# Fewer mixing steps in the second MLP's first chunk, a second load of the output blocks from SP, and a norm and two subtractions rewritten

## The chip, the cores and the metric

The kernel runs as one program on one core of a Trainium2 chip. The metric is the device time of one execution in microseconds (us); smaller is better. The engines are TensorE (PE for matmuls, PEld for its weight loads), VectorE (DVE), ScalarE (ACT), GpSimd (POOL) and SyncE (SP). DMAs are issued from SP, ACT and POOL.

## The reference

One inference step of a two-layer encoder on 512 prompt tokens and 64 sample tokens, which the kernel treats as 576 columns of one matrix with 1024 features:

```python
for i in range(2):
    h = rmsnorm(x, norm_mix[i])
    y = pool_mixer(h) if i == 0 else sparse_attention(h) @ w_o   # layer 0 pools, layer 1 attends
    x = x + y
    h = rmsnorm(x, norm_mlp[i])
    u = relu(h @ w_up[i])                # 1024 -> 4096
    x = x + (u * u) @ w_down[i]          # 4096 -> 1024
y = rmsnorm(x, norm_final)
```

Everything is float32. The two MLPs hold most of the arithmetic; the attention picks 128 or 144 keys of each query by an indexer score.

## The kernel before, in words

**Data.** `x` stays in SBUF as 8 tiles of 128 features by 576 tokens. Each float32 operand of a matmul is split into an upper part (a cast to fp32r) and a lower part (value minus upper part), and each product is three matmuls: upper by upper, upper by lower, lower by upper. A matmul takes 288 tokens (half of 576) as its moving side.

**Weights.** A weight block is a 128 by 1024 tile. `load` (L145) brings it into a staging tile `raw` of 512 KB, `split_block` casts it on ACT (L204) and subtracts on DVE or, in parts of the attention, on POOL (L205), into one of three weight tiles `w`. A `raw` tile comes free when that subtraction is done. There are two `raw` tiles, and two more in the MLPs. The list `jobs` sets the order of the loads. Loads of MLP weights are issued by SP; loads of the attention's input blocks (`in_w_in`) and output blocks (`in_w_o`) by ACT, in the order of ACT's other work.

**The MLPs.** The 4096 hidden features are handled in 4 chunks of 1024. For a chunk `c`, four `up(c, q)` calls each make two tiles of hidden features; `up(c + 1, 0)` is done ahead; then four `DownPair` calls each add two output tiles to `x`. Both the down products of most chunks and the up products of the second MLP from chunk 1 on use a seven-product scheme (Strassen-like) in place of eight. It needs sums of weight quarters. `factors` (L594 on) makes the sums of the activations. The weight sums of the first MLP are made by POOL (L278 to L283) when the block arrives; those of the second MLP are made ahead of time in DRAM, by `mixing()`.

**Mixing.** `mixing()` (L215 on) is a generator. It fills the DRAM tile `mixed` with the weight sums in 12 groups that start three steps apart; each group needs four plain copies from SP (L240: two from the weights, then two from `mixed`) and four accumulating DMAs from POOL (L234), each of 512 KB. The whole takes 3 x 12 + 9 = 45 steps. A step is taken wherever the code says `next(mixes, None)`: in the first MLP twice in each `up` with q = 1 and q = 2 and once in each DownPair with q = 1 to 3, which is 4 x (4 + 3) = 28 steps; in the second MLP six times in chunk 0's `up` calls (twice for each of q = 1, 2, 3), then once in each later `up` and in every second DownPair. The copies of a step are ordered behind the last SP load that was recorded ahead of them.

**The norms.** `Norm.stats` sums the squares over features by small matmuls (L369), and takes a square root (ACT, L388) and a reciprocal with a correction (DVE, L390 to L395) to get one factor per token; `Norm.spread` spreads the factors over the partitions: a diagonal on DVE (L359, L362), two matmuls (L349), two copies on ACT (L350) into `rbm`. The first hidden tiles wait in PSUM until `rbm` is there, and are then taken out by L713. In the first MLP `stats` stands behind the second up tile and `spread` behind the third; in the second MLP `stats` stands between the two tiles and `spread` behind the second. Matmuls at L688 then zero the two `seed` banks.

**Output blocks.** `w_o` is passed over twice: in the first pass a quarter of the tokens' products is made while the attention is still running, in the second pass (L319 on tile `wo`) the other 320 columns. Each pass loads all 8 blocks.

**Order of the work.** The program is handed to a scheduler that lays the instructions of each engine out in a fixed order before launch, by a model of its own; each engine then runs its list in that order and waits where an operand is not there.

Of the kernel before, what the change touches and what calls it, by code (L numbers as in the profile page):

```python
# [12 lines left out]
ALU = mybir.AluOpType  # L13
# [28 lines left out]
FACTORS = ("b11", "b22", "b21", "t3", "t1", "t2", "t4")  # L42
PLAIN = ((4, 4, 4, 4), (4, 0, 0, 0))
AHEAD = 2
BLOCKS = 3
VS = 2

# [2 lines left out]
def pool_dsa_kernel(ctx: ExitStack, tc: tile.TileContext, a, o):  # L50
# [114 lines left out]
    def mlp_jobs(layer, strassen, plain):  # L165
        down = a["w_down"][layer]

        def ups(c, ps):
            for q in ps:
                if q < plain[c]:  # L170
                    jobs.extend(("mlp", f) for f in rows("up", layer, c, q))
                else:
                    jobs.append(("made", "up", c, q))

        for c in range(4):
            ups(c, range(c > 0, 4))
            if c < 3:
                ups(c + 1, range(1))
            if c >= strassen:
                jobs.extend(("mlp", down[c, m]) for m in range(KT))  # L180
            elif layer:
                jobs.extend(("made", "down", c, q) for q in range(KT // 2))
            else:
                jobs.extend(("pair", *rows("down", layer, c, q)) for q in range(KT // 2))

    mlp_jobs(0, 4, PLAIN[0])
    jobs.extend(("w_in", a["w_in"][j]) for j in range(2))
    jobs.extend(("w_v", a["w_v"][j]) for j in range(2))
    jobs.extend(("w_in", a["w_in"][j]) for j in range(2, 15))
    for _ in range(2):  # L190
        jobs.extend(("w_o", a["w_o"][m]) for m in range(KT))
    mlp_jobs(1, 3, PLAIN[1])
    ready = []
    how = {"sub": dve}
# [50 lines left out]
    def loaded():  # L245

        waiting, held = [], 0
        while jobs or waiting:
            while jobs and held < LOADS_AHEAD["more" in phase] and ("last" in phase or jobs[0][0] not in ("pair", "made")):
                kind, *srcs = jobs.pop(0)  # L250
                if kind == "made":
                    r1, r2 = rows(srcs[0], 1, *srcs[1:])
                    m = mixed[:, pairs[tuple(srcs)]].rearrange("p a b -> p (a b)")
                    srcs = [r1, m[:, 1024:], m[:, :1024], r2[:, 512:]]
                mlp = kind in ("mlp", "pair", "made")
                waiting.append((kind, [load(src, src.shape[1], nc.sync if mlp else act, mlp)[:, :src.shape[1]] for src in srcs]))
                held += len(srcs)
            kind, tiles = waiting.pop(0)
            held -= len(tiles)
            yield kind, tiles  # L260
# [243 lines left out]
    def mlp(layer, gi, strassen, order=range(KT), end=None):  # L504
# [63 lines left out]
                dve.tensor_tensor(bx[j][:, 5:7, 1], t[:, 2:4], f32(bx[j][:, 5:7, 0]), ALU.subtract)  # L568
                yield

        def up_plain(order):
            w = next_block()
            pt = [psum1("up", "pd" if "pd" in phase and not ups else "po") for _ in range(2)]
            ups.append(pt)
            for n, k in enumerate(order):
                for i, (part, wt) in enumerate(((0, 0), (1, 0), (0, 1))):
                    for h in range(2):
                        pe.matmul(pt[h][:, :HT], w[:, wt, k * P:(k + 1) * P], moving(k, part, h),  # L578
                                  start=n == 0 and i == 0, stop=n == KT - 1 and i == 2)
            return pt  # L580
# [12 lines left out]
        def factors(v, u):  # L593
# [12 lines left out]
                return  # L606
            act.copy(u[:, 0:3, 0], v[:, 1:4])
            dve.tensor_tensor(u[:, 0:3, 1], v[:, 1:4], f32(u[:, 0:3, 0]), ALU.subtract)
            dve.tensor_tensor(b11, b11, b12, ALU.subtract)
            dve.tensor_tensor(b12, b12, b22, ALU.subtract)  # L610
            dve.tensor_tensor(b22, b22, b11, ALU.add)
            dve.tensor_tensor(b21, b21, b22, ALU.subtract)
            act.copy(u[:, 3:7, 0], v)
# [79 lines left out]
        def up(c, q):  # L693
# [30 lines left out]
            v = None  # L724
            if first:
                pts = []
                for i in range(2):
                    pts.append(up_plain(order))
                    if i == 1 - layer:
                        norm.stats(banks[0])  # L730
                late.append(pts)
                if layer:
                    spread()
                return
            for i in range(2):
                pt = up_plain(range(KT))
                if late:
                    spread()
                if not i:
                    v = new_v()  # L740
                evacuated(i, pt)
                if layer or q in (1, 2):
                    next(mixes, None)
                if layer:
                    with tc.issue_after(last_of["diag"].ins), tc.issue_after(last_of["rt"].ins):
                        next(mixed, None)
                if not layer and (c, q) == (3, 3):
                    us[c][q] = us[c][q] or u_tile()
                    factors_by_tile(i, v, us[c][q])
# [7 lines left out]
        for c in range(4):  # L757
            for q in range(c > 0, 4):
                up(c, q)
            if c < 3:  # L760
                up(c + 1, 0)
            if c < strassen:
                for q in range(KT // 2):
                    if q % 2 if layer else q:
                        next(mixes, None)
                    pair = DownPair(q, us[c], seeded(), layer > 0)
                    pair.opening(c == 3 and q == 0)
                    pair.closing((c, q) != (3, 3))
                continue
# [793 lines left out]
```

## Time and profile before

| | us |
|---|---|
| median of 3 runs | 1120.58 |
| lowest, highest of them | 1118.39, 1123.9 |
| the profiled execution | 1127.65 |
| its span, first to last instruction | 1125.9 |
| PE busy in the span | 1091.3 (97%) |
| DVE, ACT, POOL busy | 790.7, 557.7, 293.6 |

In the span of the profiled execution the up matmuls of the first MLP run from 36 to 387 us, the attention's input projections from about 440 on, the second pass of the output blocks from 694 to 726 us, and the second MLP from 726 us to the end; the up matmuls of its first chunk end at 779 us. A view of stretches gives the busy time of each engine in each stretch, and then the clock that was granted to TensorE as a share of full speed, the busy share of the 16 DMA engines, and what they moved in GB/s.

### The profile page before, as it was taken

The page shows a single profiled execution, that of the slowest core. Times are in us where ns is not written, and L with a number is a line of the kernel's source. Part 1 is how long each engine was busy: PE and PEld are TensorE (multiplying, and loading weights), DVE is VectorE, ACT ScalarE, POOL GpSimd, SP SyncE. Part 2 cuts the span into 40 slices and gives each one's busy share as a digit, 9 for nine tenths or more (in the row PEclk, how much of TensorE's full clock was granted, in tenths as well). Part 3 has the DMA queues.
Part 4 walks back from the last instruction along what each step waited for, and adds up shares of the span by engine and source line. Part 5 has one row for each costly group of instructions (what it writes and reads, how often), then busy time and mean ns, then how long its engine had stood idle before and what let it go on. Part 6 is the DMA issues. An engine that isn't in the chain of part 4 may idle for free. (4 is left out here: it accounts for less than half of the span.)

```text
span 1125.9 us, 20515 instructions
## 1 busy us (share of the span) xinstructions
PE 1091.3 (97%) x8118; PEld 1073.9 (95%) x8118; DVE 790.7 (70%) x1448; ACT 557.7 (50%) x937; POOL 293.6 (26%) x227
## 2 busy tenths in 40 slices
PE   9999999999999999999899999999899999999995
PEld 8999999999999999999789998999799999999995
DVE  7767656766755886659999942887567867865644
ACT  8534334334434454435387654655436636644542
POOL 3004414431351560147973440002000000000002
PEclk9999999999999999999999997999999999999997
DMA  6264488389469867457642341458977565555402
GB/s 218 61 177 105 129 225 237 90 225 256 117 158 263 215 184 235 119 144 194 196 118 67 118 128 37 146 154 241 274 208 213 167 199 161 167 154 174 141 20 84
DMA packets 80208, 183.52 MB, mean 163 GB/s; under 512 B 10753, under 2 KB 22320, under 8 KB 80112
## 3 DMA queue, kind: packets, MB, share of 16 engines
q1 hardware_dynamic: 62304, 139.71, 38.6%
q0 software_dynamic: 13056, 25.17, 13.7%
q10 hardware_dynamic: 4752, 17.34, 5.0%
q8 instruction: 64, 1.05, 0.4%
q14 instruction: 32, 0.26, 0.1%
HBM read 167.10 MB, written 61.22 MB: 203 GB/s over the span
## 5 line engine op out<-in xcount | busy, mean ns | idle before, releaser
L204 ACT CAST w<-raw 128x1024 fp32r<-128x1024 f32 (+2 forms) x242 | 211.2, 890 | 234.4 <-PE seed L422 73.8
L205 DVE TENSOR_TENSOR w<-raw,w 128x1024 fp32r<-128x1024 f32 (+2 forms) x224 | 244.6, 1099 | 68.9 <-ACT w L204 68.6
L578 PE MATMUL up<-xs,w 128*128 128x288 f32 x1536 | 205.8, 295 | 0.5 <-DVE v L713 0.5
L578 PEld LDWEIGHTS up<-xs,w 128*128 128x128 f32 x1536 | 203.8, 188 | 0.9 <-DVE v L713 0.9
L422 PE MATMUL seed<-u,w 128*128 128x288 f32 x1008 | 146.7, 296 | 2.1 <-ACT seed L447 1.2
L422 PEld LDWEIGHTS seed<-u,w 128*128 128x128 f32 x1008 | 138.2, 188 | 3.5 <-ACT seed L447 1.9
L422 PE MATMUL a<-u,w 128*128 128x288 f32 x672 | 101.5, 298 | 6.2 <-ACT w L204 4.5
L422 PE MATMUL c<-u,w 128*128 128x288 f32 x672 | 100.7, 297 | 2.0 <-DVE w L205 1.2
L422 PEld LDWEIGHTS a<-u,w 128*128 128x128 f32 x672 | 93.8, 189 | 8.0 <-ACT w L204 5.4
L422 PEld LDWEIGHTS c<-u,w 128*128 128x128 f32 x672 | 93.1, 188 | 3.2 <-DVE w L205 1.7
L319 PE MATMUL pj<-xs,w 128*128 128x288 f32 x672 | 92.8, 294 | 0.0
L319 PEld LDWEIGHTS pj<-xs,w 128*128 128x128 f32 x672 | 90.4, 188 | 0.7
L234 POOL DMA_DIRECT2D mixed<-in_w_down x24 | 27.6, 1196 | 173.2 <-DMA mixed<-mixed 128.7
L234 POOL DMA_DIRECT2D mixed<-in_w_up x24 | 27.5, 1207 | 140.6 <-DMA mixed<-mixed 121.3
L422 PE MATMUL seed<-bx,w 128*128 128x288 f32 x432 | 63.0, 298 | 0.0
L807 POOL TENSOR_TENSOR x<-x,spare 128x320 f32<-128x320 f32 (+1 forms) x9 | 8.2, 945 | 208.8 <-ACT spare L803 208.8
L422 PEld LDWEIGHTS seed<-bx,w 128*128 128x128 f32 x432 | 59.9, 190 | 0.1
L205 DVE TENSOR_TENSOR w<-sum,w 128x1024 fp32r<-128x1024 f32 (+1 forms) x32 | 33.4, 1044 | 33.1 <-ACT w L204 33.1
L278 POOL TENSOR_TENSOR sum<-raw 128x512 f32<-128x512 f32 x16 | 23.5, 1470 | 123.4 <-DMA raw<-in_w_down 123.4
L319 PE MATMUL dn<-u,w 128*128 128x288 f32 (+2 forms) x384 | 51.7, 295 | 0.0
L713 DVE SCALAR_TENSOR_TENSOR v<-up,rbm 128x288 f32<-128x288 f32 x80 | 32.5, 450 | 27.2 <-PE up L578 27.1
L319 PEld LDWEIGHTS dn<-u,w 128*128 128x128 f32 x384 | 51.0, 188 | 0.2
(292 smaller groups left out, 1974.6 us busy)
## 6 DMA issues: line engine op xcount, KB each, us to landing
raw<-in_w_up SPq DMA_DIRECT2D x52, 512.0 KB, 4.6
raw<-in_w_down SPq DMA_DIRECT2D x52, 512.0 KB, 4.5
raw<-mixed SPq DMA_DIRECT2D x48, 512.0 KB, 4.1
mixed<-in_w_down POOLq DMA_DIRECT2D x24, 512.0 KB, 7.6
mixed<-mixed SPq DMA_DIRECT2D x24, 512.0 KB, 7.9
mixed<-in_w_up POOLq DMA_DIRECT2D x24, 512.0 KB, 10.0
raw<-in_w_o ACTq DMA_DIRECT2D x16, 512.0 KB, 3.6
raw<-in_w_in ACTq DMA_DIRECT2D x15, 512.0 KB, 4.3
```

Of the source, the lines that this page charges most:

```text
L204: act.copy(w[:, 0, at], src[:, at])
L205: how["sub"].tensor_tensor(w[:, 1, at], src[:, at], f32(w[:, 0, at]), ALU.subtract)
L234: pool.dma_start(to, add, accum_op=ALU.add)
L278: pool.tensor_tensor(s[:, :512], r2[:, :512], r2[:, 512:], ALU.add)
L319: pe.matmul(pt[h][:, :m] if isinstance(pt, tuple) else pt[:, h, :m], wt, xs[k][:, part, c:c + m], start=(k == ks[0] and i == 0), stop=(k = ...
L422: pe.matmul(bank[:, :HT], wt[:, at], ut, start=first and j == 0 and i == 0, stop=j == 3 and i == 2, skip_group_check=True)
L578: pe.matmul(pt[h][:, :HT], w[:, wt, k * P:(k + 1) * P], moving(k, part, h), start=n == 0 and i == 0, stop=n == KT - 1 and i == 2)
L713: dve.scalar_tensor_tensor(v[:, 2 * i + h], pt[h][:, :HT], 0.0, halves(norm.rb)[:, h], ALU.max, ALU.mult)
L807: pool.tensor_tensor(x[k][:, t], x[k][:, t], rb, ALU.mult)
```

## The change

It has five parts.

- In `up`, a step of mixing is taken once in every plain `up` with q = 1, 2 or 3, and once more with q = 1 and 2 in the first MLP only. The first MLP has 4 x (5 + 3) = 32 steps in place of 28, the second MLP's first chunk three in place of six in its `up` calls. The 45 steps in all stay.
- The second pass of the output blocks has a kind of its own, `w_o2`, whose loads are issued by SP.
- `stats` now stands in the second up tile of both MLPs (ahead of its fourth of 8 parts in the first MLP, ahead of its first in the second MLP), and `spread` behind that tile in both.
- In `factors` of the second MLP, `b11 -= b12` and `b12 -= b22` are one instruction on a view of two tiles.
- The place of `up(c + 1, 0)` comes from a table, `UP_BEFORE`, whose entries name the place at which it stood.

```diff
+UP_BEFORE = ((0, 0, 0, None), (0, 0, 0))
+STATS = (3, 0)
...
-    for _ in range(2):
-        jobs.extend(("w_o", a["w_o"][m]) for m in range(KT))
+    for kind in ("w_o", "w_o2"):
+        jobs.extend((kind, a["w_o"][m]) for m in range(KT))
...
-                mlp = kind in ("mlp", "pair", "made")
+                mlp = kind in ("mlp", "pair", "made", "w_o2")
...
+                if between and n == between[0]:
+                    between[1]()
...
-            dve.tensor_tensor(b11, b11, b12, ALU.subtract)
-            dve.tensor_tensor(b12, b12, b22, ALU.subtract)
+            back, ahead = (bass.AP(t.tensor, t.offset, [t.ap[0], (step * HT, 2), t.ap[1]]) for t, step in ((b11, -1), (b12, 2)))
+            dve.tensor_tensor(back, back, ahead, ALU.subtract)
...
+                stats = lambda: norm.stats(banks[0])
                 for i in range(2):
-                    pts.append(up_plain(order))
-                    if i == 1 - layer:
-                        norm.stats(banks[0])
+                    pts.append(up_plain(order, (STATS[layer], stats) if i else None))
                 late.append(pts)
-                if layer:
-                    spread()
+                spread()
...
-                if late:
-                    spread()
...
-                if layer or q in (1, 2):
+                if (i == 0 and q) or (not layer and q in (1, 2)):
                     next(mixes, None)
```

Three places show what the scheduler made of it. Rows give the line, the operation, and output and inputs; the changed kernel's line numbers are one to three off.

**SP and POOL, the second MLP's first chunk.** SP before, from the last load for `up(1, 0)` to the first down pair's loads (`raw` is a staging tile, `mixed` the DRAM tile):

```order
L145 DMA raw_8560<-in_w_up 128x512
L240 DMA mixed<-mixed 128x2x512
L240 DMA mixed<-in_w_up 128x2x512 x2
L240 DMA mixed<-mixed 128x2x512 x2
L240 DMA mixed<-in_w_up 128x2x512 x2
L145 DMA raw_8989<-mixed 128x1024
L145 DMA raw_8985<-in_w_down 128x1024
L145 DMA raw_8987<-mixed 128x1024
L240 DMA mixed<-mixed 128x2x512
```

The same stretch of SP with the change:

```order
L147 DMA raw_8569<-in_w_up 128x512
L241 DMA mixed<-in_w_up 128x2x512 x2
L241 DMA mixed<-mixed 128x2x512 x2
L147 DMA raw_8987<-mixed 128x1024
L147 DMA raw_8983<-in_w_down 128x1024
L147 DMA raw_8985<-mixed 128x1024
L147 DMA raw_8989<-in_w_down 128x512
```

Four copies stand ahead of the first down pair's loads in place of seven, and none between its loads. POOL before, from the end of the attention to the last norm:

```order
L1447 TENSOR_TENSOR x_7967<-x_7967,wo_7323 128x256 x2
L234 DMA mixed<-in_w_down 128x2x512 x2
L234 DMA mixed<-in_w_up 128x2x512 x3
L234 DMA mixed<-in_w_down 128x2x512
L234 DMA mixed<-in_w_up 128x2x512 x7
L807 TENSOR_TENSOR x_7964<-x_7964,spare_11802 128x320 x2
```

With the change:

```order
L308 TENSOR_TENSOR ck_7799<-raw_7801,ck_7799 128x512
L1446 TENSOR_TENSOR x_7978<-x_7978,wo_7334 128x256 x2
L235 DMA mixed<-in_w_down 128x2x512
L235 DMA mixed<-in_w_up 128x2x512 x7
L806 TENSOR_TENSOR x_7975<-x_7975,spare_11792 128x320 x2
```

The second MLP is left with 8 accumulating DMAs in place of 13; the other five are in the first MLP.

**ACT and PE, the first MLP's norm.** ACT before (`rt` the square roots, `rbm` the spread factors, `v` the hidden tiles):

```order
L204 CAST w_715<-raw_356 128x1024
L204 CAST w_789<-raw_361 128x1024
L388 ACTIVATE rt_118_774<-seed_656,eps 128x4
L388 ACTIVATE rt_118_774<-seed_656,eps 64x1
L204 CAST w_874<-raw_658 128x1024
L350 COPY rbm_126_845<-seed_656 128x288
L350 COPY rbm_126_845<-seed_657 128x288
L714 ACTIVATE v_850<-v_850 128x576 x2
```

With the change:

```order
L205 CAST w_715<-raw_356 128x1024
L389 ACTIVATE rt_118_744<-seed_656,eps 128x4
L389 ACTIVATE rt_118_744<-seed_656,eps 64x1
L205 CAST w_813<-raw_361 128x1024
L351 COPY rbm_122_790<-seed_656 128x288
L351 COPY rbm_122_790<-seed_657 128x288
L717 ACTIVATE v_795<-v_795 128x576 x2
L205 CAST w_874<-raw_658 128x1024
```

One cast has gone behind the square roots, one behind the copies of `rbm`. On PE the two spreading matmuls were directly ahead of the matmuls that zero the seeds:

```order
L578 MATMUL up_793<-xs_606,w_660 128x288
L349 MATMUL seed_656<-diag_842,ones 128x288
L349 MATMUL seed_657<-diag_842,ones 128x288
L688 MATMUL seed_656<-s_95_607,ones 128x288
L688 MATMUL seed_657<-s_95_607,ones 128x288
```

With the change fourteen matmuls of the third up tile stand between; these are the spreading matmuls and the first three of the fourteen:

```order
L350 MATMUL seed_656<-diag_787,ones 128x288
L350 MATMUL seed_657<-diag_787,ones 128x288
L581 MATMUL up_816<-xs_604,w_660 128x288
L581 MATMUL up_817<-xs_604,w_660 128x288
L581 MATMUL up_816<-xs_605,w_660 128x288
```

**ACT and SP, the second pass of the output blocks.** ACT before, near the attention's end (`pT`, `ck`, `p`, `ot` are the attention's tiles):

```order
L145 DMA raw_7981<-in_w_o 128x1024
L1304 COPY pT_7754<-pt_7753 128x512
L1305 COPY pT_7754<-pt_7753 64x128
L306 CAST ck_7788<-raw_7790 128x512
L1257 ACTIVATE p_7762,sums_970_7513<-p_7762,nm_7768 128x576
L145 DMA raw_8014<-in_w_o 128x1024
L204 CAST w_7983<-raw_7981 128x512 x2
L1304 COPY pT_7795<-pt_7794 128x512
```

SP with the change; the first of these loads is the one that stood first on ACT above:

```order
L147 DMA raw_7992<-in_w_o 128x1024
L1444 DMA x_7978<-xd 128x1152
L147 DMA raw_8025<-in_w_o 128x1024
L147 DMA raw_8058<-in_w_o 128x1024
L147 DMA raw_8091<-in_w_o 128x1024
```

ACT keeps its casts and copies in the same order, without the DMAs. On SP the loads stand among the attention's last loads and ahead of the second MLP's.

More of the change, by code (lines that the diff above doesn't have):

```diff
@@ L176, in mlp_jobs @@
             ups(c, range(c > 0, 4))
-            if c < 3:
-                ups(c + 1, range(1))
             if c >= strassen:
                 jobs.extend(("mlp", down[c, m]) for m in range(KT))
[L181 to L184, printed above, removed]
+                continue
+            for q in range(KT // 2):
+                if q == UP_BEFORE[layer][c]:
+                    ups(c + 1, range(1))
+                jobs.append(("made", "down", c, q) if layer else ("pair", *rows("down", layer, c, q)))
     mlp_jobs(0, 4, PLAIN[0])
@@ L569, in mixing, with up_plain @@
                 yield
-        def up_plain(order):
+        def up_plain(order, between=None):
             w = next_block()
@@ L759, in mlp @@
                 up(c, q)
-            if c < 3:
-                up(c + 1, 0)
             if c < strassen:
                 for q in range(KT // 2):
+                    if q == UP_BEFORE[layer][c]:
+                        up(c + 1, 0)
                     if q % 2 if layer else q:
```

## The prediction

> **What bounds the kernel now.** I read the page's busy times first, then the chain that ended last and the stretches, then PE's waits stage by stage.
>
> ```profile
> span 1125.9 us, 20515 instructions
> PE 1091.3 (97%) x8118; PEld 1073.9 (95%) x8118; DVE 790.7 (70%) x1448; ACT 557.7 (50%) x937; POOL 293.6 (26%) x227
> ```
>
> PE is busy for 1091.3 of 1125.9 us, and nothing in the change takes a matmul away. So only two things can be won: the 34.6 us in which PE does nothing, a part of which is the start and the end of the program, and the time in which its clock is held down. The question is which of these gaps the change reaches. The largest one in the second MLP is in its first chunk, where the chain reads
>
> ```profile
> 769.82 21.23 DMA raw<-in_w_down
> ...
> 791.07 1.05 ACT w L204
> ...
> 793.40 9.18 DMA raw<-in_w_down
> ...
> 805.32 0.80 PE a L422 x4
> ```
>
> (start and length in us). Twice PE waits for a block of the first down pairs, and the block waits for its load: 21.23 us and 9.18 us for 512 KB. The page's list of DMAs has what such a load usually takes (its last number, the median):
>
> ```profile
> raw<-in_w_down SPq DMA_DIRECT2D x52, 512.0 KB, 4.5
> ```
>
> The stretches around it show why, and what it costs (length; busy time of PE, PEld, DVE, ACT, POOL; granted clock; busy share of the DMA engines; GB/s):
>
> ```profile
> 760.00:780.00 20.00, 20.00 (x152) 19.89 (x151) 16.27 (x30) 11.09 (x15) 5.65 (x5) 1.00 0.82 228
> 780.00:806.00 26.00, 21.30 (x140) 20.04 (x139) 15.70 (x21) 12.41 (x18) 3.38 (x3) 0.93 1.09 273
> 806.00:850.00 44.00, 44.00 (x332) 44.00 (x332) 27.00 (x41) 17.78 (x23) 2.27 (x2) 1.00 0.76 223
> ```
>
> From 780 to 806 us the DMA engines are full (1.09), PE is idle for 26.00 - 21.30 = 4.7 us, and the clock falls to 0.93 of full speed, which over 26 us is 0.07 x 26 = 1.8 us of work. On both sides PE has no gap. What fills the DMA engines are the copies that SP issues ahead of the load:
>
> ```profile
> 762.95 0.57 SPq L240 DMA_DIRECT2D mixed<-mixed  x1
> 763.57 1.27 SPq L240 DMA_DIRECT2D mixed<-in_w_up  x2
> 764.94 1.54 SPq L240 DMA_DIRECT2D mixed<-mixed  x2
> 766.53 2.12 SPq L240 DMA_DIRECT2D mixed<-in_w_up  x2
> ...
> 769.82 0.34 SPq L145 DMA_DIRECT2D raw<-in_w_down  x1
> ```
>
> Seven mixing copies go out within 6 us, and the down block's load stands behind them. In the whole chunk (736 to 812 us) the tile `mixed` is written by
>
> ```profile
> L240 SPq DMA_DIRECT2D mixed<-mixed x6: 550/564/883, 737.3 to 802.1; - x6
> L234 POOL DMA_DIRECT2D mixed<-in_w_up x6: 1126/1126/1133, 770.2 to 798.4; - x6
> L240 SPq DMA_DIRECT2D mixed<-in_w_up x4: 610/797/1097, 763.6 to 767.6; - x4
> L234 POOL DMA_DIRECT2D mixed<-in_w_down x3: 1126/1138/1172, 742.9 to 776.9; - x3
> ```
>
> that is by 10 copies and 9 accumulating DMAs.
>
> **Part by part.** *Mixing in the second MLP.* By the order of the rows, 4 copies stand ahead of the first down block in place of 7, none between its loads, and the second MLP has 5 accumulating DMAs fewer. Over the chunk it is 5 copies in place of 10, so some 10 transfers of 0.524 MB, or 5.2 MB, go. At the 273 GB/s of the full stretch that is 19 us of DMA time. How much is needed? PE's own waits in the chunk (total, times, longest) are
>
> ```profile
> PE a L422 <- ACT w L204: 3.3, 2, 2.4
> PE a L422 <- DVE w L205: 1.5, 2, 0.7
> ```
>
> The longest of each, 2.4 + 0.7 = 3.1 us, belong to the first load, which landed at 791.05: it has to land 3.1 us sooner. The three copies that no longer stand ahead of it are 1.57 MB, 5.8 us at that rate, and fewer accumulating DMAs run beside it. The second load, issued at 793.40, is 9.18 - 4.5 = 4.7 us shorter at the median length, and only the remaining 1.7 us of waits are its. I take the whole gap as gone, 4.7 us idle and 1.8 us of clock: **-6.5 us**. The least it can bring is nothing, if another wait steps in; more than 6.5 us cannot be had here, since the stretches before and after have no gap.
>
> [...] Idle stretches of 2.4 us and less came with a granted clock of 0.93. [...]
>
> *Mixing in the first MLP.* Its four more steps have to be paid for. All 45 steps are 96 transfers, so four are about 8.5 transfers, or 4.5 MB, in this stretch:
>
> ```profile
> 100.00:430.00 330.00, 326.45 (x2440) 324.20 (x2439) 225.61 (x316) 136.24 (x169) 128.78 (x92) 1.00 0.70 186
> ```
>
> The DMA engines have room on average (0.70). PE loses 330.00 - 326.45 = 3.55 us here beside 28 steps; in proportion four more cost 3.55 x 4/28 = **+0.5 us**. I take that because most steps cost PE nothing today. It can hardly bring a gain, since the mixing is not on PE's path there; the other end is the price of the slower case below. The rows it goes by are those of POOL's queue, in which the accumulating DMAs (L234) and the sums for the first MLP's down blocks (L278 to L283) stand in one order (from 44 to 430 us, and ACT's waits from 72):
>
> ```profile
> POOL mixed L234 <- DMA mixed<-mixed: 48.3, 6, 14.4
> ACT w L204 <- POOL sum L283: 42.4, 15, 5.1
> ```
>
> *The norms.* In the first MLP PE waits twice at the norm:
>
> ```profile
> PE seed L688 <- ACT rbm L350: 0.5, 1, 0.5
> PE up L578 <- DVE v L713: 0.5, 1, 0.5
> L578 PE MATMUL up<-xs,w 128*128 128x288 f32 x1536 | 205.8, 295 | 0.5 <-DVE v L713 0.5
> ```
>
> With the change fourteen up matmuls stand between the spreading matmuls and the zeroing ones. At 205.8 us for 1536 (last row, of the groups of instructions) a matmul of this kind is 0.134 us from one to the next, so they give 1.9 us of cover, and the copies of `rbm` are no longer behind a weight cast on ACT. Both waits go: **-1.0 us**. Two casts move back on ACT. The block of the next up tile, `w_715`, is still cast ahead of the norm; the two that moved are for the fifth and sixth tiles, one and two tiles of 48 matmuls (6.4 us each) later, and that covers them. If the cover failed, a cast (1.05 us in the chain above) and a subtraction of about its length would show, some 2 us; so the range here is -1.0 to +2. In the second MLP `stats` keeps its place on PE between the two tiles, and PE's waits of that chunk, quoted above, have none for it: nothing.
>
> *Output blocks from SP.* The place where they could matter is the attention's end:
>
> ```profile
> 669.34 1.26 POOL w L205
> ...
> 670.62 4.74 DMA raw<-in_w_o
> 671.02 0.59 ACT L1304 COPY pT<-pt 128x512 f32<-128x512 f32 x1 [2.60 <-POOL w L205]
> 669.00:695.00 26.00, 24.68 (x144) 22.61 (x143) 8.65 (x27) 12.68 (x34) 4.73 (x5) 0.74 0.26 84
> ```
>
> ACT stands idle for 2.60 us because a DMA in its list waits for a `raw` tile that POOL frees at 669.34 + 1.26 = 670.60; behind it a copy of `pT` waits that the attention needs. On SP the same load waits for the same tile, is issued at the same 670.6 and lands at the same 675.4, and the cast of it stands ahead of the next `pT` copy on ACT as before. ACT gains 2.6 us of which the chain uses nothing, for that gate is further on. What stands behind the load on SP is the last load of `x`, issued in the trace before at 670.72, and then the next output blocks; none is late by it. I take **0**. The bounds are wide: PE is idle for 26.00 - 24.68 = 1.3 us here and runs at 0.74 of full speed, 6.8 us of clock. If the released ACT kept PE denser, up to 8 us could be won; if PE's work is thinned out further, the same could be lost in part.
>
> *Two subtractions as one.*
>
> ```profile
> L610 DVE TENSOR_TENSOR v<-v 128x288 f32<-128x288 f32 x10 | 4.6, 457 | 0.3
> L609 DVE TENSOR_TENSOR v<-v 128x288 f32<-128x288 f32 x10 | 4.5, 454 | 0.1
> L337 DVE TENSOR_TENSOR u<-u 128x576 f32<-128x576 f32 x1 | 0.8, 752 | 0.0
> ```
>
> The pair takes 911 ns, an instruction of the joint size 752 ns: ten times 0.16, 1.6 us of DVE time in the second MLP. PE's waits there are for weight casts, not for these: 0 now, and at most -1.6 if DVE were the bound. Were the new view slower by half of 752 ns, ten of them would cost DVE 2.2 us more than the pairs, hidden by the same matmuls. The table `UP_BEFORE` moves nothing.
>
> **Sum.** -6.5 + 0.5 - 1.0 + 0 + 0 = -7.0 us, against the profiled execution: 1127.65 us, of which 1125.9 span, becomes 1120.7. That execution is 7.1 us above the median of the runs, so something in it is larger than in a usual run. The trace offers two events of that size, this stall (6.5) and the slow clock at the attention's end (6.8). If it is the second, the sum holds for the median: 1120.58 - 7.0 = **1113.6 us**.
>
> **Rivals.** *The stall is smaller in the runs that count, or comes back elsewhere.* For it: the 7.1 us just named, of which the stall may be a part. Against it: ten transfers of 512 KB in one chunk are there in every run, and 19 us of DMA time in a chunk that is full is no small excess. With a quarter of the 6.5 us left to win the change is -1.6 + 0.5 - 1.0 = -2.1: 1118.5 us.
>
> *The first MLP pays: slower.* One mechanism: the step that now stands at the end of each chunk's up calls puts an accumulating DMA into POOL's queue ahead of the pair sums, it waits for its copy, and the sums, the blocks made from them and PE wait with it. Such a wait on `mixed` is 48.3 / 6 = 8.1 us today, and ACT already waits for the last sum 15 times, up to 5.1 us. If about 5 us of the wait are covered (that longest wait leaves PE running), 3.1 us a chunk show on PE in four chunks: +12.4. It decides when the copy on SP lands after the down blocks' raw loads. With the rest that is -7.5 + 12.4 = +4.9, about 1125.5, and above that with some lost clock, 1127. Against it: groups start three steps apart, so a step's transfers mostly wait for things of steps ago, and PE waits little in this stretch now.
>
> *The attention's end moves out of the slow clock.* The 6.8 us are won besides: 1113.6 - 6.8 = 1106.8. The row of ACT speaks for it, the unmoved gate against it.
>
> **How the numbers follow.** The forecast has 0.53, the smaller stall 0.28, the first MLP's price 0.10, the attention's gain 0.09. A change of this kernel of 0.5%, 5.6 us, is about what can be told from none, so the border of faster is 1115.0 us and of slower 1126.2. The forecast's own range is 1110 to 1118, from 3 us more by the clock to the norm's +2 and a part of the stall left; about 0.36 of the 0.53 lies below 1115.0, the rest is no change. The smaller stall is no change, the attention's gain faster. Of the first MLP's price 0.07 are slower and 0.03 no change. That makes faster 0.45, no change 0.48, slower 0.07. The range has to take in the smaller stall and a bit of the attention's gain: 1108 to 1121.
>
> **What would show it.** Right: in the second MLP's first chunk the load of the first down block lands within some 10 us, PE has no gap up to the end of the chunk, and the clock stays at 1.00; the two waits at L688 and L578 near 63 us are gone; PE's lost time from 100 to 430 us stays below 5 us; ACT's 2.60 us idle time behind POOL's subtraction is gone while the gate at the output block's landing remains. Wrong: POOL waits on `mixed` and ACT on L283 grow in the first MLP and PE's gaps there with them; or the down blocks' loads still take over 9 us; or the stretch from 669 to 695 us shows another clock than 0.74, which would move the time by more than the rest of the change.

## The result, and the profile after

The changed kernel takes 1114.32 us (median of 5 runs, 1111.97 to 1115.79). The kernel before, run beside it, takes 1123.49 us (5 runs, 1118.39 to 1125.69). The ratio is 0.9925 with an interval of 0.9896 to 0.9955: the change gains 0.45 to 1.04%. The forecast was 1113.6 us.

The profiled execution of the changed kernel takes 1113.53 us, 14.1 us less than that of the kernel before. Of these, 5.8 us are not a gain of the median: the half clock at the attention's end, which the prediction showed in the row 0.74, comes in some executions only (a granted clock as low as 0.983, the value of that execution, is found in 12 of 127 executions of kernels that load the second pass's output blocks from ACT, and with a time to match in none of 47 of kernels that load them from SP). Only one of these 12 was profiled; that the others hold the same event is not shown, and nine of them take 1129 to 1132 us, further above the median than this event.

The first two lines of the page after:

```profile
span 1111.8 us, 20521 instructions
PE 1084.1 (98%) x8118; PEld 1070.1 (96%) x8118; DVE 789.6 (71%) x1438; ACT 558.0 (50%) x937; POOL 294.4 (26%) x227
```

The view of stretches of the kernel after (length; busy time of PE, PEld, DVE, ACT, POOL; granted clock; busy share of the DMA engines; GB/s). The first three answer to the stretches of the second MLP's first chunk, the fourth to the attention's end, the last two are the first MLP's start, with the norm, and its main part:

```profile
760.00:780.00 20.00, 20.00 (x149) 19.79 (x149) 15.54 (x25) 11.32 (x17) 4.52 (x4) 1.00 1.06 276
780.00:806.00 26.00, 26.00 (x197) 26.00 (x196) 19.48 (x27) 12.31 (x16) 0.00 (x0) 1.00 0.55 166
806.00:850.00 44.00, 44.00 (x332) 44.00 (x331) 28.54 (x39) 22.36 (x31) 2.27 (x2) 1.00 0.73 206
669.00:695.00 26.00, 26.00 (x204) 24.69 (x203) 9.02 (x31) 14.03 (x39) 5.19 (x6) 1.00 0.26 85
40.00:100.00 60.00, 60.00 (x448) 59.35 (x449) 41.78 (x67) 25.64 (x33) 10.77 (x8) 1.00 0.58 149
100.00:430.00 330.00, 325.95 (x2439) 324.00 (x2438) 225.50 (x316) 137.38 (x170) 136.32 (x96) 1.00 0.74 200
```

From 780 to 806 us PE is busy for 26.00 us where it was 21.30, at full clock: the stall is gone. From 100 to 430 us PE is busy for half a microsecond less than before.

SP's own work ahead of the first down pair, in order of time (start and length in us):

```profile
755.88 0.33 SPq L147 DMA_DIRECT2D raw<-in_w_up  x1
756.26 1.26 SPq L241 DMA_DIRECT2D mixed<-in_w_up  x2
757.56 1.28 SPq L241 DMA_DIRECT2D mixed<-mixed  x2
760.47 0.33 SPq L147 DMA_DIRECT2D raw<-mixed  x1
763.13 0.33 SPq L147 DMA_DIRECT2D raw<-in_w_down  x1
768.60 0.32 SPq L147 DMA_DIRECT2D raw<-mixed  x1
```

Four copies go out where seven did. The load issued at 763.13 answers to the one of 769.82 in the kernel before. The DMA view of that instant has

```profile
raw<-in_w_down SPq DMA_DIRECT2D x1, 512.0 KB, 9.2
```

so 9.2 us from issue to landing in place of 21.23.

To see where the time went, I divided both profiled executions at PE's marks. From the last matmul on an up tile of the second MLP's first chunk to the first matmul on a `dn` tile (the last chunk's plain down products) it was 278.94 us and is 271.51 (-7.4); from the attention's first `sc` matmul to the first of the output blocks' second pass it was 139.42 and is 133.66 (-5.8, the event just named); from the first up matmul to the attention's first projection it was 397.06 and is 395.74 (-1.3). The other parts agree within 0.3 us.

### The profile page after: what moved, and what is told of

It is laid out like the page before. It is cut to its first block, busy times and chain, and to the rows that moved or that the text cites. A ratio compares the mean times of both kernels' runs of the same rounds, so it can differ in the third digit from the quotient of the medians.

```text
span 1111.8 us, 20521 instructions
## 1 busy us (share of the span) xinstructions
PE 1084.1 (98%) x8118; PEld 1070.1 (96%) x8118; DVE 789.6 (71%) x1438; ACT 558.0 (50%) x937; POOL 294.4 (26%) x227
## 3 DMA queue, kind: packets, MB, share of 16 engines
q8 instruction: 64, 1.05, 0.4%
## 4 chain that ended last, share of the span: by engine, by line
PE 61%; DVE 8%; DMA 4%; POOL 3%; issue 2%; ACT 2%; SPq 0%; DVEq 0%; POOLq 0%; ACTq 0%
PE seed L423 14%; PE c L423 9%; PE a L423 9%; PE up L581 6%; PE pj L320 4%; PE dn L320 4%; PE o L1316 3%; DVE w L206 2%; PE wa L320 2%; PE wo L320 2%; PE sc L1277 2%; PE pt L1297 1%; DVE work L1241 1%; PE v L1110 1%; DVE m L1240 1%
## 5 line engine op out<-in xcount | busy, mean ns | idle before, releaser
L205 ACT CAST w<-sum 128x1024 fp32r<-128x1024 f32 (+1 forms) x32 | 26.7, 834 | 54.8 <-POOL sum L284 47.1
```

The costliest lines, as they stand in the source:

```text
L205: act.copy(w[:, 0, at], src[:, at])
```

## The experiments

Medians are given with the number of executions, and the ratio to the kernel before, run in the same comparison. The kernel before had 1121.97 us in the first comparison (23 executions), 1121.25 in the second (24) and 1120.15 in the third (19). The ratio on record is not the quotient of the two medians. In the first comparison, where the kernel before took 1129 to 1132 us in six of its 23 executions, that quotient lies nearer to 1 than the ratio: 0.9985 for the output blocks, 0.9933 and 0.9912 for the two mixing rules.

My theory after the result (M) was that the mixing in the second MLP is the whole gain. The rival (S) was that loading the output blocks from SP also frees the attention's end from its slow clock, as the 5.8 us in the profile suggest.

### Output blocks from SP alone

The kernel before with one edit:

```diff
-    for _ in range(2):
-        jobs.extend(("w_o", a["w_o"][m]) for m in range(KT))
+    for kind in ("w_o", "w_o2"):
+        jobs.extend((kind, a["w_o"][m]) for m in range(KT))
...
-                mlp = kind in ("mlp", "pair", "made")
+                mlp = kind in ("mlp", "pair", "made", "w_o2")
```

> Kernel before with one edit: the second pass of the output blocks is loaded by SP. Theory M (the gain is the mixing in the second MLP, as predicted; this edit is worth nothing): within 1 us of before, the landing of the output block at the attention's end still the gate, granted clock near 0.74 from 669 to 695 us. Theory S (this edit also closes PE's gap of 1.3 us at the attention's end and keeps the clock up there): 5 to 8 us faster than before, no PE gap near 678 us, no half clock between 669 and 695 us.

Measured: 1120.32 us (12), ratio 0.9962 (0.9929 to 0.9995). This is 1.6 us under the median beside it, and 0.3 us from that of the first three runs, 1120.58. The half clock of the attention's end is not in its profile, the stall in the second MLP is. What S expected of the profile is there, what it expected of the time is not; M's "within 1 us" is missed by 0.6 us, and its clock near 0.74 did not come. The interval just leaves out 1, so a gain of some tenths of a per cent is not excluded.

### The new mixing rule alone, in both MLPs and in the second only

```diff
-                if layer or q in (1, 2):
+                if (i == 0 and q) or (not layer and q in (1, 2)):
```

> Kernel before with one edit: the new rule for mixing steps in both MLPs (32 steps in the first, three in the up calls of the second MLP's first chunk). Theory M: 6 us faster (6.5 from the stall in the second MLP's first chunk, 0.5 back in the first MLP), with no PE gap near 790 us. Theory S: the same place gains, but 6 us of the change's 9 come from elsewhere, so about 3 us faster or less.

Measured: 1114.44 us (6), ratio 0.9897 (0.9855 to 0.9939). One line gives the time of the whole change. The stall is gone, and the attention's end runs at full clock in this profile although ACT loads the output blocks. So that clock is not the SP edit's alone.

With the first MLP's 28 steps kept, the rule is

```diff
-                if layer or q in (1, 2):
+                if (i == 0 and q) if layer else q in (1, 2):
```

> Kernel before with three mixing steps in place of six in the up calls of the second MLP's first chunk, and the first MLP's 28 steps as before (the three steps are made up later in the second MLP). Theory M: 6.5 us faster, all of the stall gone. If the first MLP's share of the copies mattered, this one is faster than the run with both by 0.5 us or more; if the steps made up later collide with other loads, a PE gap shows after 806 us.

Measured: 1112.14 us (6), ratio 0.9877 (0.9835 to 0.992), 2.3 us under the kernel with both. The intervals overlap; the profiles say more. PE's waits from 100 to 430 us in the kernel with the new rule in both MLPs begin with

```profile
PE seed L422 <- ACT seed L441: 1.6, 1, 1.6
```

and in the one with 28 steps there is only a gap of 0.33 us at that place (388 us). What makes this wait is shown further on.

### The norm alone

`stats` and `spread` moved as in the change, nothing else:

```diff
-                    pts.append(up_plain(order))
-                    if i == 1 - layer:
-                        norm.stats(banks[0])
+                    pts.append(up_plain(order, (STATS[layer], stats) if i else None))
...
-                if layer:
-                    spread()
+                spread()
...
-                if late:
-                    spread()
```

> Kernel before with one edit: stats and spread amid and behind the second up tile. Both theories: the two PE waits near 63 us go, 1.0 us faster (0.1%), not to be told from no change by the times; the trace shows it. The order of everything behind stays, so the stall near 790 us stays at 4 to 5 us of idle PE.

Measured: 1119.75 us (12), ratio 0.9974 (0.9937 to 1.0011). The time can't tell 0.9 us from nothing, the stretch can. Its row, where the kernel before has PE busy for 59.08 us:

```profile
40.00:100.00 60.00, 60.00 (x449) 59.22 (x449) 41.81 (x67) 25.63 (x33) 10.24 (x8) 1.00 0.50 132
```

The two waits of 0.46 us are gone, 0.92 us.

### The change without its SP edit, without its mixing, and with the first MLP's 28 steps

Each is the changed kernel with one part undone; the diffs are those above, backwards (for the last, the rule of the second MLP only).

> The changed kernel with the output blocks' second pass loaded from ACT again. Theory M, the gain is the mixing's: 1114 to 1115, within 1 us of the changed kernel, ACT's idle time behind POOL's subtraction is back and PE does not wait for it. Theory S, SP's loads bring the attention's end its full clock: 1117 to 1121, and the half clock near 680 us is in the profile again.

Measured: 1114.06 us (7), ratio 0.9934 (0.9909 to 0.9959). As with the SP edit, and as M expected; the full clock is there in the profile without SP's loads.

> The changed kernel with the old rule for the steps of mixing. Theory M: 1119 to 1121, the stretch from the last up tile of the second MLP's first chunk on is 278 to 281 us again in place of 271.5, with the waits for the first down pair's blocks and a half clock of 3.4 us. Theory S: 1114 to 1116, since the other parts bring most of the gain.

Measured: 1118.16 us (12), ratio 0.9971 (0.9945 to 0.9998). Slower than the change by 3.8 us and faster than the kernel before by 3.1, a little better than M expected; S's 1114 to 1116 does not hold. Its profile has the stall, without the half clock that M expected: PE's waits and two stretches there are

```profile
PE a L423 <- ACT w L205: 3.0, 2, 1.6
PE a L423 <- DVE w L206: 0.7, 1, 0.7
PE seed L423 <- ACT seed L448: 0.7, 1, 0.7
...
780.00:796.00 16.00, 11.55 (x79) 10.40 (x78) 10.60 (x14) 8.28 (x11) 1.13 (x1) 1.00 1.09 273
796.00:800.00 4.00, 4.00 (x32) 4.00 (x31) 2.05 (x3) 1.86 (x3) 0.00 (x0) 1.00 1.07 313
```

Here 4.45 us of idle PE left the clock at 1.00. The clock's share of the stall is so a part that comes or not: from 770 to 830 us the granted clock is 0.97 in the kernel before and with the output blocks from SP alone, 0.94 with the norm alone, and 1.00 here. That may be a part of why this kernel lies under the expected 1119.

> The changed kernel, with the 28 steps of mixing in the first MLP kept (the second MLP's first chunk has its three). Theory A, the four extra steps cost the first MLP about 2 us (in the profiles this stretch was 397.6 us with them and 395.4 us without, and there was a wait of 1.6 us at its end with them): the time is 1.5 to 2.2 us below the changed kernel's 1114.3, so 1112 to 1113, and the wait of 1.6 us is gone. Rival, the extra steps cost 0.5 us as predicted and the 2 us belong to single executions: 1113.8, and the wait may stay.

Measured: 1113.19 us (6), ratio 0.9921 (0.9895 to 0.9947). The wait of 1.6 us is gone, 0.68 us stay, but the time can't be told from the change's. The 1.5 to 2.2 us that I expected were too much; over all profiles the cost is 1 us (below). By the intervals, no kernel of this study is shown to be faster than the changed one.

### Two subtractions as one, alone

```diff
-            dve.tensor_tensor(b11, b11, b12, ALU.subtract)
-            dve.tensor_tensor(b12, b12, b22, ALU.subtract)
+            back, ahead = (bass.AP(t.tensor, t.offset, [t.ap[0], (step * HT, 2), t.ap[1]]) for t, step in ((b11, -1), (b12, 2)))
+            dve.tensor_tensor(back, back, ahead, ALU.subtract)
```

> The kernel before with the two subtractions as one, nothing else. Both theories: the joint subtraction takes about 0.75 us in place of 0.91 for the pair, ten times, and the time is that of the kernel before, within 0.8 us. A rival, DVE is what the second MLP waits for: 1.6 us less.

Measured: 1121.44 us (12), ratio 1.001 (0.9992 to 1.0029): nothing. The group of the joint subtraction takes what was worked out, 753 ns:

```profile
L610 DVE TENSOR_TENSOR v<-v 128x576 f32<-128x576 f32 x10 | 7.5, 753 | 0.1
```

### What makes the stall: the number of copies, their place, or the full DMA engines

Three steps in the chunk, but as late as can be, in the kernel before:

```diff
-                if layer or q in (1, 2):
+                if (q == 3 or q == 2 and i) if layer else q in (1, 2):
```

> The kernel before, with three steps of mixing in the second MLP's first chunk as in the change, but taken as late as they can be (the last of the third up call and both of the fourth), so that five copies in a row stand ahead of the first down load, none between the loads. The first MLP keeps 28 steps. If the number of steps in the chunk decides: no stall, 1112 to 1113 as with the three spread steps. If the copies in a row ahead of the load decide: the first down load takes over 10 us, PE waits 1 to 3 us for it, 1114 to 1117.

Measured: 1113.75 us (12), ratio 0.9936 (0.9912 to 0.996), with no wait of PE in the stretch:

```profile
770.00:830.00 60.00, 60.00 (x450) 59.79 (x449) 41.15 (x60) 28.23 (x36) 7.13 (x7) 1.00 0.91 244
```

Five copies in a row stand ahead of the loads. The first load behind them is issued at 766.25 and takes

```profile
raw<-mixed SPq DMA_DIRECT2D x1, 512.0 KB, 11.9
```

In the kernel before, the same first load, behind seven copies at 768.76, takes

```profile
raw<-mixed SPq DMA_DIRECT2D x1, 512.0 KB, 19.7
```

and 9.0 us behind four in the kernel after. Over all profiles this load takes 7.0 to 9.0 us behind four copies (eight profiles) and 18.2 to 20.9 behind seven (five). So copies ahead of a load on SP do lengthen it, and PE bears 12 us without a wait. One more thing sets the kernel before apart. SP's own waits there (755 to 806 us) contain

```profile
SPq L240 <- DMA mixed<-in_w_up: 9.1, 1, 9.1
```

The eighth copy, which stands between the loads of the first pair, waits 9.1 us for an accumulating DMA, and what stands behind it in SP's list waits with it:

```profile
784.81 0.55 SPq L240 DMA_DIRECT2D mixed<-mixed  x1
785.46 8.28 SPq L145 DMA_DIRECT2D raw<-in_w_down  x2
```

All five profiled kernels with the old rule in the second MLP have this wait (8.0 to 9.1 us), and none of the nine with the new or the late one has it. But PE's two waits for a block in this trace do not follow from it. The load that ends the first gap went out at 769.82, ahead of the held copy, and took its 21.23 us behind the seven copies (19.5 to 21.6 us in the five profiles). Of the two loads in the last row, the first is a block of 256 KB; the second, which ends the second gap, went out at 793.40. The chain shows what it waited for:

```profile
792.15 1.23 DVE w L205
793.38 0.03 DVE v L610
793.40 9.18 DMA raw<-in_w_down
```

It went out as DVE's subtraction of the late first block ended, which frees a `raw` tile. So both gaps go back to the load behind the seven copies. Whether the held copy lengthens the second load's 9.18 us is not shown.

The last rival is the one that the prediction leaned on, the load of the DMA engines. To the kernel with three steps in the second MLP I added nine copies within DRAM, issued by POOL:

```diff
+    extra = dram.tile([P, 18, 512], F32, name="extra")
...
-                        pool.dma_start(to, add, accum_op=ALU.add)
+                        last_of["pool"] = pool.dma_start(to, add, accum_op=ALU.add)
+            for k in range(9) if n == 31 else ():
+                with tc.issue_after(last_of["pool"].ins):
+                    pool.dma_start(extra[:, 2 * k:2 * k + 2], sources(k)[0])
```

> The kernel before with the second MLP's first chunk at three steps of mixing (first MLP 28 steps), and nine copies of 512 KB within DRAM, whose result is not used, issued by POOL behind the accumulating DMAs near 765 us, in place of the transfers that went away. SP's list is that of the kernel without these copies. If the DMA engines' load made the stall: the down blocks' loads take 9 to 15 us again, PE waits 2 to 5 us between 770 and 805 us, 1115 to 1119. If the copies ahead of the loads in SP's queue made it: no wait of PE there, 1111 to 1113.5 as without the extra copies.

Measured: 1113.46 us (6), ratio 0.9943 (0.9923 to 0.9963). The stretches, then the added copies of the stretch from 755 to 800 us, and a load of `mixed` issued at 766.65, when four of the added copies had just gone out (the last number is the median time to landing):

```profile
760.00:780.00 20.00, 20.00 (x150) 19.79 (x149) 15.09 (x25) 11.06 (x16) 8.59 (x12) 1.00 1.05 305
780.00:806.00 26.00, 26.00 (x197) 25.95 (x197) 18.09 (x27) 12.01 (x15) 2.47 (x3) 1.00 1.02 328
...
extra<-in_w_down POOLq DMA_DIRECT2D x6, 512.0 KB, 16.7
extra<-in_w_up POOLq DMA_DIRECT2D x3, 512.0 KB, 17.3
...
raw<-mixed SPq DMA_DIRECT2D x1, 512.0 KB, 7.1
```

The DMA engines are about as busy as in the stall (1.02 here, 1.09 there) and move more, 328 in place of 273 GB/s; the added copies take 17 us each. The load of 766.65 takes 7.1 us, and 6.9 in the kernel without the added copies. Later loads do get longer: the median of six loads of `mixed` is 8.4 us with the copies and 5.8 without, and the one down block of 512 KB whose landing is on record in both takes 9.3 and 3.6. The traffic's side expected that, but PE does not wait once. So this much traffic beside the loads did not make the stall: it belongs to the copies that stand ahead of the loads in SP's list. (The first added copy went out at 764.17, 3 us behind the first down block's load, whose own landing is not on record.)

### The half clock at the attention's end

Two of the profiled kernels have it, the kernel before and the one with the late steps, both with ACT's loads; the others with ACT's loads don't. I compared DVE's subtraction of the output block that PE needs next with POOL's additions to `x`. In the kernel before (first two rows) and with the late steps (last two), start, length, and the idle time before with what ended it:

```profile
676.14 2.12 DVE L205 TENSOR_TENSOR w<-raw,w 128x512 fp32r<-128x512 f32 x2 [2.56 <-ACT w L204]
675.84 1.86 POOL L1447 TENSOR_TENSOR x<-x,wo 128x256 f32<-128x256 f32 x2 [2.15 <-DMA x<-xd]
```

```profile
675.52 1.97 DVE L205 TENSOR_TENSOR w<-raw,w 128x512 fp32r<-128x512 f32 x2 [2.89 <-ACT w L204]
675.07 1.86 POOL L1447 TENSOR_TENSOR x<-x,wo 128x256 f32<-128x256 f32 x2 [2.33 <-DMA x<-xd]
```

and in the kernel after

```profile
675.54 1.29 DVE L206 TENSOR_TENSOR w<-raw,w 128x512 fp32r<-128x512 f32 x2 [1.37 <-ACT w L205]
676.35 1.76 POOL L1446 TENSOR_TENSOR x<-x,wo 128x256 f32<-128x256 f32 x2 [3.28 <-DVE w L206]
```

Where POOL starts first, the subtraction takes 2 us in place of 1.29, and DVE's next work for the attention, on which PE waits for 1.0 to 1.1 us, is late. In these two profiles the last load of `x`, for which POOL waits, goes out 0.1 us after the block's load; in the twelve others it goes out 0.4 to 1.3 us after it, the least with both in SP's list being 0.4. The block itself lands later in the same two: 4.7 and 5.1 us after its issue, in place of 3.4 to 3.7 in the twelve others. Theory P was that the overlap of POOL and DVE is the cause. To force it, I let POOL do three additions more ahead of the last pair in the changed kernel, and, as a control, behind it:

```diff
+            for k in range(3 if m == 6 else 0):
+                pool.tensor_tensor(ahead[k], ahead[7], ahead[7], ALU.add)
             pool.tensor_tensor(x[m][:, :2 * P], x[m][:, :2 * P], ahead[m], ALU.add)
```

> The changed kernel with three further additions on POOL (128x256 each, their results are not used) ahead of the attention's last pair of additions to x, so that POOL is surely busy while DVE subtracts the block that PE needs next. Theory P, the half clock at the attention's end comes when POOL's additions and that subtraction overlap: the subtraction takes 1.9 to 2.1 us in place of 1.29, PE waits about 1 us near 677 us, the clock is at half for some 13.65 us after it, and the time is 6 to 9 us above the changed kernel's 1114.3, so 1120 to 1123, although SP loads the blocks. Rival, the half clock belongs to a late load and POOL's work has no part in it: 1113 to 1115.5, full clock from 669 to 695 us.

Measured: 1112.41 us (6), ratio 0.9938 (0.9917 to 0.9959). The rows of its trace:

```profile
673.40 2.16 DVE L206 TENSOR_TENSOR w<-raw,w 128x512 fp32r<-128x512 f32 x2 [0.67 <-ACT w L205]
672.80 2.20 POOL L1447 TENSOR_TENSOR wo<-wo 128x256 f32<-128x256 f32 x3 [1.18 <-DVE wo L1372]
...
669.00:695.00 26.00, 26.00 (x201) 24.68 (x200) 9.40 (x30) 13.84 (x39) 5.25 (x7) 1.00 0.24 85
```

The overlap lengthens the subtraction as foreseen, from 1.29 to 2.16 us. But PE does not wait, and the clock stays: in this execution the block was there earlier (it landed 3.5 us after its issue), so that the long subtraction ended at 675.56, in the kernel before at 678.26. My 1120 to 1123 was wrong.

> The changed kernel with the same three further additions on POOL behind the attention's last pair of additions to x. Theory P: the subtraction takes 1.29 us as before, since the additions stand behind it, 1113 to 1116; should they meet one of the next subtractions of a block, another wait of PE and a half clock would show at that place. Rival, more work on POOL costs by itself: the same as with the additions ahead.

Measured: 1113.89 us (6), ratio 0.9945 (0.9922 to 0.9968), the subtraction at 1.29 us, as expected.

So the overlap with POOL (0.87 us of lengthening) does not make the event alone. In the two profiles that have it, the block also lands 1 us later, and both go with the load of `x` that follows 0.1 us behind the block's. That the two together make the gap is read from these profiles; it was not produced by an experiment. Whether the SP edit keeps the event away stays open: the counts in the result speak for it, and the later load of `x` would be the way, but the two kernels that differ in nothing else (the change with and without it) have the same time.

## Why the prediction was right

**The stall in the second MLP, -6.5 us.** Right, and a little too small: 7.4 us in the profiles' stretch. Between the same marks the five profiles with the old rule take 276.3 to 280.8 us and the nine without it 271.4 to 271.5, so the stall is in every one of the five and costs 4.8 to 9.3 us, 6.9 in the mean. The signs named came: the first down block lands in 9.2 us, PE has no gap to the end of the chunk, the clock is 1.00. (The 9.2 us are "within some 10 us", but also "over 9 us", which stood among the signs of being wrong; the two overlapped.) The clock was taken from a mean of 0.93 over 26 us, 1.8 us; what the trace has are 3.4 us at half clock, 1.7 us, which agrees. With the gaps of 4.7 us that is 6.4. The last 1.0 us lies at the edges of the four gaps, which the sum left out: the view counts the last matmul as busy for 0.29 us, while matmuls here start 0.13 us apart, and the second start after a gap comes 0.24 us behind the first; that is some 0.25 us a gap. The reason was right in one half. "Seven mixing copies go out within 6 us, and the down block's load stands behind them" holds. That the DMA engines are full (1.09) holds too, but it is not the cause: with the engines at 1.02 to 1.05 there is no stall when the copies are on POOL's queue. The working by bytes and GB/s (19 us of DMA time less) gave no term of the sum, only the belief that the whole gap goes; the same belief could have been had from SP's list.

**The clock after a short gap.** By the row I counted 1.8 us of clock to the stall, and the clock is 1.00 without it. The stretches of the kernel before show the half clock behind short gaps at both places:

```profile
669.00:680.90 11.90, 10.57 (x83) 9.68 (x82) 5.68 (x15) 6.04 (x16) 4.73 (x5) 1.00 0.54 172
681.00:694.60 13.60, 13.60 (x60) 12.43 (x59) 2.98 (x12) 6.15 (x18) 0.00 (x0) 0.50 0.02 7
...
790.00:793.60 3.60, 0.70 (x3) 0.47 (x4) 1.45 (x2) 1.34 (x2) 0.00 (x0) 1.00 1.10 270
793.62:797.00 3.38, 3.38 (x15) 3.38 (x15) 2.49 (x6) 2.00 (x2) 0.00 (x0) 0.50 1.11 242
```

Gaps of 2.37 and 0.73 us with 0.5 us of work between them are followed by 3.4 us at half clock, and single gaps of 0.19 and 1.14 us by 13.6 us. A gap of that size is not enough by itself: the kernel without the mixing had 1.40, 0.73, 0.71 and 1.61 us and kept its clock (1.00). What decides between the two stays open.

**The first MLP's steps, +0.5 us.** Too small by half a microsecond. Over nine profiles with 28 steps PE loses 1.75 to 4.96 us between 100 and 430 us, 2.96 in the mean; over five with 32 steps 3.90 to 4.29, 4.02 in the mean: +1.06. The ranges overlap, in one profile with 28 steps. The cost is not in proportion to the steps: most of it is one wait. PE's waits from 100 to 430 us after begin with

```profile
PE seed L423 <- ACT seed L442: 1.6, 1, 1.6
```

at 389 us, the end of the last chunk's up calls; it is 1.4 to 1.8 us in all five kernels with 32 steps, and with 28 it is 0.2 to 0.7 us or not there. The chain to it in the kernel after reads

```profile
370.33 13.03 DMA mixed<-mixed
...
383.89 1.14 POOL mixed L235
385.02 1.32 POOL sum L284
...
386.37 0.63 ACT w L205
...
389.17 0.31 ACT seed L442
```

This is the mechanism that the prediction gave to its slower rival: an accumulating DMA stands in POOL's list ahead of a pair sum and waits for its copy, and the sum, the cast of the block and PE wait with it. All five kernels with 32 steps have this chain there; in the SP edit alone and the new rule in the second MLP only, with 28 steps, the chain at this place has no POOL in it. It shows once, in the last chunk, and not in all four, and with it PE loses about 1 us more than with 28 steps, not 12.4. So the rival's price did not come, but the step that failed in the forecast's +0.5 is the share by steps: it priced an even loss, and what came was one wait behind POOL's queue. "PE's lost time stays below 5 us" holds (4.05). POOL's and ACT's rows (44 to 430 us, and ACT's from 72) are

```profile
POOL mixed L235 <- DMA mixed<-mixed: 43.3, 7, 12.9
ACT w L205 <- POOL sum L284: 47.1, 15, 5.6
```

48.3 us of waiting for copies within `mixed` became 43.3, but POOL's waits for the transfers into `mixed` from the weights went from 44.0 and 10.4 us to 52.0 and 15.8, and ACT's waits for a sum from 42.4 to 47.1. These are the signs that the prediction named for the slower case, in a small form.

**The norms, -1.0 us.** Right: -0.92 us, both waits gone, and the moved casts show nowhere.

**Output blocks from SP, 0.** Right for the median as far as can be told, with the undoing and the doing alone as witnesses (1114.06 against 1114.32, and 1120.32 against 1121.97, whose ratio just leaves out 1). The reason had an error of reading: I took the row of 0.74 as the kernel's, with a gate (the block's landing) that the change does not move, and named a clock other than 0.74 as a sign of being wrong. The clock is 1.00 after, and ACT's cast still waits for the block's landing (2.25 us); the row of 0.74 was of that execution. The size read from it, 6.8 us of clock beside 1.3 us of idle PE, was too large too: the stretch of the attention became 5.8 us shorter. The prediction did see that the profiled execution held "something larger than in a usual run" and took the right one of two events, which is why 1120.58 - 7.0 was the right sum. Its ground, that the transfers are there in every run, is borne out by the five profiles with the stall.

**Two subtractions as one, 0.** Right: 1.001 (0.9992 to 1.0029).

**The sum.** -7.4 + 1.06 - 0.92 = -7.3 us against the forecast of -7.0: the stall's and the first MLP's errors cancel, which is luck. With the stall's mean of 6.9 it is -6.8. From 1120.58 that is 1113.3 or 1113.8; measured 1114.32. The kernel before had 1123.49 us in the run beside it, so the difference of the medians is 9.2 us, and the interval of the ratio, 5 to 12 us, takes in all three. The forecast counts from 1120.58, the median of three runs; the medians of the kernel before lay between 1120.15 and 1123.49 in this study, so part of how near the time came is luck too. The smaller stall (1118.5), the first MLP's price (1125.5) and the attention's gain (1106.8) were no better; the first would have been the time with a quarter of the stall's gain.

## What to carry to other kernels

Before explaining a late load by busy DMA engines, read what stands ahead of it in its own queue, and that queue's own waits, and then follow the chain to see which of them PE's gap goes back to: here it was the copies ahead and not the copy that held the queue for 9 us. Traffic of 328 GB/s in place of 273, with the added copies on POOL's queue, cost PE nothing. A cost that is shared out evenly over the steps of a background task misses the one step that stands ahead of work that PE needs. Where a profiled execution is longer than the median, find which event makes it so, before its rows are used as the kernel's. Background work of one stage is best spread with the loads' slack in view: three steps in that chunk were free at two different places, six were not.

## What the runs showed of the hardware

A load of 512 KB on SP takes 4.3 us in the median (of down blocks, kernel after), 7.0 to 9.0 us behind four copies, 11.9 behind five and 18.2 to 20.9 behind seven, while with nine copies on POOL beside them, at 305 to 328 GB/s in all, loads of `mixed` took 8.4 us in the median. DVE's subtraction of two 128x512 halves takes 1.29 us where POOL's additions start behind it and 1.97 to 2.16 us where they start ahead of it. And in the kernel before PE's clock went to half (0.50) for 13.6 us after gaps of 0.19 and 1.14 us amid matmuls of 64 to 288 columns (30 of the 59 from 672 to 681 us have 64), which I had not expected; in the changed kernel without its mixing it stayed at 1.00 after 4.45 us of gaps in four pieces within 16 us.
